# One expert's weights ahead: reordering the expert stage of a two-layer diffusion backbone, and reading its weights in longer runs

## The chip, the cores and the metric

The kernel runs on one core of one Trainium2 chip. The metric is the device time of one execution in microseconds (us). Three timed runs of the kernel before gave 2632.49, 2635.15 and 2641.01 us, a median of 2635.15 us.

## The reference, cut to what matters

Two layers work on 256 latent and 256 context tokens of width 1024. Each layer is a token mixer (differential attention, a long convolution, windowed attention, merged by gates) followed by a mixture of 16 experts. In the second layer only the 256 latent tokens go through the expert part. Each expert picks its 32 highest-scoring tokens per stream, and the expert part is:

```
def ec_moe(h, p):
    B, N, D = h.shape
    cap = CAPACITY_FACTOR * N // N_EXPERTS          # 32
    aff = softmax(h @ router_w)                     # N x 16
    g, idx = lax.top_k(swapaxes(aff, 1, 2), cap)    # per expert
    xg = take_along_axis(h, idx)                    # 16 x 32 x 1024
    a = einsum('becd,edf->becf', xg, moe_w1)
    b = einsum('becd,edf->becf', xg, moe_w3)
    y = einsum('becf,efd->becd', silu(a) * b, moe_w2) * g
    return zeros_like(h).at[flat].add(y)
```

All weights are float32. One expert has three matrices of 1024 x 1024, 12.6 MB, so a layer reads 201 MB of expert weights and the program 403 MB of its 590 MB.

## The kernel before, in words

A Python planner writes every engine's instructions in a fixed order. Foreground work (the mixer's 116 weight blocks, then the experts) is written in program order; background tasks (attention heads, convolutions, the filter of the long convolution, the modulation vectors) are generators whose steps are put between foreground matmuls when a cost model says that their inputs are ready. A `yield wait(...)` ends a step and names what the next one needs; its `gate` keeps a task back until a condition holds, for instance until a pool of tiles has a free buffer (`room`).

**Mixers.** For each block of 128 output columns TensorE does 24 matmuls of 128x512 (float32r, high and low halves). Modulation vectors 3 and 4 (shift and scale ahead of the experts) come out of background tasks, laid out as `mod[p, v, k, s]` with model row k*128+p on partition p. `router_prep` then multiplies the router weights by them.

**Ahead of the experts.** `post` transposes each of the 8 column blocks of the new hidden state to token rows (`p`), and ScalarE, VectorE and GpSimd split it into three bfloat16 parts `xr`. `gather` selects an expert group's tokens with one-hot matmuls from `xr` and gives `xg[g]`, whose partition is the position inside a block of 128 model rows.

**Experts.** In layer 0 there are two token streams, M = 64 rows per expert, NC = 2 column halves of N = 512 that share the systolic array; in layer 1 M = 32, NC = 4, N = 256. `prod` runs one product: for each of 8 blocks k of 128 model rows, NC matmuls into one PSUM tile. `expert(e)` is a chain: product with w1, silu on ScalarE into `s1`; product with w3, multiply on VectorE into `s1`; transposes of `s1` on TensorE; a copy to `aT` on VectorE; product with w2; copies of the result to `yS`. Between the matmuls of `prod` side work is written: `gather` of the next group of four experts and `scatter` of the last group, and in layer 0 from expert 5 on the filter of layer 1's long convolution.

**Weights.** `moe` cuts each matrix into two chunks of 2 MB, in the order w1, w3, w2 of each expert. A chunk holds four blocks k, and partition p of block k holds weight row k*128+p: one 4 KB row at a time, four rows 512 KB apart. `fill` issues chunks on the SP queue as long as fewer than `room` of them are held (6 at first in layer 0, 4 while the filter runs, 7 in layer 1), and is called again when `prod` has used up a chunk. A few chunks are put together from smaller buffers (`extra`, and every seventh in layer 1), with a DMA for each row block or pair. The last expert's w2 is cut by columns instead, so that its result ends in pieces.

Of the kernel before, what the change touches and what calls it, by code (L numbers as in the profile page):

```python
# [408 lines left out]
class Kernel:  # L409
# [344 lines left out]
    def mod_post(self, l, v):  # L754
        yield wait(self.modc[l][:, v])
        if v in (1, 4):
            self.mod_G(l, v)
        if v == 4:
            yield wait(self.modc[l][:, 4])
            self.router_prep(l)  # L760
            yield wait()
# [38 lines left out]
    def router_prep(self, l):  # L800
# [12 lines left out]
        self.gw[l], self.cr[l] = gw, cr  # L813

# [33 lines left out]
    def filter(self, task, l):  # L848
# [37 lines left out]
        for c0 in range(0, D, W):  # L886
# [11 lines left out]
            yield wait(ab[0])  # L898
# [8 lines left out]
            for j, op in enumerate((OP.add, OP.subtract)):  # L907
# [14 lines left out]
                yield wait(w3, dec) if j else wait()  # L922
# [123 lines left out]
    def turn(self, w, task):  # L1046
# [9 lines left out]
        return o  # L1056

# [195 lines left out]
    def hyena_gen(self, task, l, cs, u3):  # L1253
# [5 lines left out]
        yield wait(uv, gate=lambda: l in self.K and len(self.dft or ()) == 2 and self.room(a2=2)())  # L1259
        p = self.bank([128, 2, ns, 128])  # L1260
# [4 lines left out]
        uh = self.sb("a2", [128, 2, ns * 128], F32R, name="uh")  # L1265
        ul = self.sb("a2", [128, 2, ns * 128], F32R, name="ul")
# [54 lines left out]
        for j, (sa, a) in enumerate(ys):  # L1321
            yield wait(a, bank=0, gate=None if j else self.room(a2=5))
            if j == 0:
                Yf = [[self.sb("a2", [128, 2, ns * 128], F32R, name="yf") for _ in range(2)] for _ in range(2)]
            yh, yl = Yf[j]
            c = self.sb("a2", [128, 2, ns * 128], name="yc")
# [45 lines left out]
    def mixer(self, l):  # L1372
# [102 lines left out]
        def swa_in():  # L1475
            for j in range(2):
                def ev_sv(p, j=j):
                    if j == 0:
                        self.svready = set()
                        self.svt = [self.sb("a2", [128, 4, 128], name="svt") for _ in range(2)]  # L1480
# [4 lines left out]
            for g in range(2):  # L1485
                def ev_sk(p, g=g):
                    r = self.sb("a2", [128, 512], name="sk")
# [84 lines left out]
    def post(self, l, k, nq):  # L1572
# [8 lines left out]
        xr = [x[:, :, z] for x in self.xr]  # L1581
        d = self.sb("a2", [128, nq, 128], name="xd")
# [10 lines left out]
        self.acopy(xr[0], p)  # L1593
        self.tt(d, p, xr[0], OP.subtract)
# [4 lines left out]
    def moe(self, l):  # L1599
# [8 lines left out]
        chunks = []  # L1608
        for e in range(NE):
            for n in ("moe_w1", "moe_w3", "moe_w2"):  # L1610
                v = A[n][l, e].rearrange("(k p) n -> p k n", p=128)
                for hf in range(2):
                    if e == NE - 1 and n == "moe_w2":
                        chunks.append(v[:, :, hf * 512:hf * 512 + 512])
                    else:
                        chunks.append(v[:, hf * 4:hf * 4 + 4, :])
# [3 lines left out]
        extra = {4: (4, 0, 1), 7: (3, 2, 2)} if l < L - 1 else {5: (4, 0, 1), 7: (3, 2, 2)}  # L1620

        def fill(room, more=0):
            while len(self.mw) < len(chunks):
                i = len(self.mw)
                c = chunks[i]
                if i in extra:
# [4 lines left out]
                    for k in range(len(t)):  # L1631
                        nc.sync.dma_start(t[k], c[:, k])
                    if extra[i][1]:
                        t.append([self.sb("a2", [128, 512], name="mw") for _ in range(2)])
                        base += t[-1]
                        for h in range(2):
                            nc.sync.dma_start(t[-1][h], c[:, 3, h * 512:h * 512 + 512])
                elif self.held >= room:
                    return
                elif l == L - 1 and (i == 6 or i > 7 and i % 7 == 0):  # L1640
                    x = [self.sb("a8", [128, 2, D], name="mw")] + [self.sb("a4", [128, D], name="mw") for _ in range(2)]
                    nc.sync.dma_start(x[0], c[:, 0:2])
                    for k in range(2):
                        nc.sync.dma_start(x[1 + k], c[:, 2 + k])
# [6 lines left out]
                else:  # L1651
                    x = self.sb("a16", list(c.shape), name="mw")
                    nc.sync.dma_start(x, c)
# [7 lines left out]
        def body():  # L1661
# [124 lines left out]
            def prod(out, st, ws, free=True):  # L1786
                n = out.shape[1]
                m = len(ws[0])
                for k in range(KT):
# [7 lines left out]
                    if k % SIDE or not aside():  # L1797
                        self.bg.pump(0.25)

            def expert(e):  # L1800
                g, j = divmod(e, 4)
                st = lambda k: xg[g][k // 4][:, k % 4, j, :]
                w = self.mw[6 * e:6 * e + 6]
                a = self.bank([128, N])
                prod(a, st, w[0:2])
                s1 = self.sb("a2", [128, N], name="s1")
                nc.scalar.activation(s1, a, AF.Silu)
                b = self.bank([128, N])
                w = self.mw[6 * e:6 * e + 6]
                prod(b, st, w[2:4])  # L1810
                self.tt(s1, s1, b, OP.mult)
                aside()
# [181 lines left out]
```

## Time and profile before

| what | value |
|---|---|
| median of three timed runs | 2635.15 us |
| the profiled execution, and its span | 2637.57 us, 2635.8 us |
| TensorE busy | 2232.3 us, 85% of the span |
| VectorE, ScalarE, GpSimd busy | 1334.5, 883.4, 790.4 us |
| HBM read | 584.66 MB, 223 GB/s over the span |
| mean granted TensorE clock | 0.947 |

The profile page is one execution. Its span is the time from the first to the last instruction. The page cuts the span into 40 slices of 66 us; in each it gives the busy tenths of every engine, the granted TensorE clock, the busy share of the 16 DMA engines and what they moved. The same can be asked for any stretch of time; the sections below call this the table by stretches. The program has four stages: mixer 0 until about 1000 us, experts of layer 0 until 1515 us, mixer 1 until 2147 us, experts of layer 1 until the end.

### The profile page before, as it was taken

The page shows a single profiled execution, that of the slowest core. Times are in us where ns is not written, and L with a number is a line of the kernel's source. Part 1 is how long each engine was busy: PE and PEld are TensorE (multiplying, and loading weights), DVE is VectorE, ACT ScalarE, POOL GpSimd, SP SyncE. Part 2 cuts the span into 40 slices and gives each one's busy share as a digit, 9 for nine tenths or more (in the row PEclk, how much of TensorE's full clock was granted, in tenths as well). Part 3 has the DMA queues.
Part 4 walks back from the last instruction along what each step waited for, and adds up shares of the span by engine and source line. Part 5 has one row for each costly group of instructions (what it writes and reads, how often), then busy time and mean ns, then how long its engine had stood idle before and what let it go on. Part 6 is the DMA issues. An engine that isn't in the chain of part 4 may idle for free.

```text
span 2635.8 us, 38658 instructions
## 1 busy us (share of the span) xinstructions
PE 2232.3 (85%) x14938; PEld 1528.6 (58%) x14938; DVE 1334.5 (51%) x2899; ACT 883.4 (34%) x1933; POOL 790.4 (30%) x775
## 2 busy tenths in 40 slices
PE   6999898989989998998999799889888886656565
PEld 4777666767768774333343277777777763222223
DVE  4777778787672324223442068777888541111111
ACT  4445344555452242101110055545545330000001
POOL 2643435532233530001110055564554420000000
PEclk8999999999999999999999999999999988888887
DMA  8444333121213367999999953332466789999997
GB/s 292 118 118 120 93 102 114 49 59 55 64 57 95 90 247 306 373 402 404 357 376 405 400 171 89 97 88 73 118 181 190 192 309 409 409 409 409 408 409 302
DMA packets 390239, 590.31 MB, mean 224 GB/s; under 512 B 45948, under 2 KB 278056, under 8 KB 388776
## 3 DMA queue, kind: packets, MB, share of 16 engines
q1 hardware_dynamic: 390056, 587.84, 62.8%
q8 instruction: 118, 1.93, 0.3%
q14 instruction: 65, 0.53, 0.1%
HBM read 584.66 MB, written 3.15 MB: 223 GB/s over the span
## 4 chain that ended last, share of the span: by engine, by line
PE 51%; DVE 19%; DMA 19%; issue 4%; ACT 4%; SPq 2%; POOL 1%; DVEq 0%; ACTq 0%; POOLq 0%
PE p L458 47%; DMA mw<-in_moe_w_dram 16%; DVE arena L261 6%; DVE t L261 5%; PE p L469 3%; DVE wl L261 2%; SPq L261 2%; DMA wm<-in_w_mod_dram 2%; DVE qp L261 1%; ACT arena L261 1%; ACT wh L261 1%; DVE yb L261 1%; DVE yc L261 1%; DVE ma L261 1%; POOL wl L261 1%
## 5 line engine op out<-in xcount | busy, mean ns | idle before, releaser
L458 PE MATMUL p<-mw,xg 128*32 128x256 f32 (+1 forms) x3072 | 403.3, 508 | 120.5 <-DMA mw<-in_moe_w_dram 120.0
L458 PE MATMUL p<-hhi,wl 128*128 128x512 f32 (+1 forms) x1344 | 480.6, 358 | 28.0 <-DVE wl L261 27.7
L458 PE MATMUL p<-hhi,wh 128*128 128x512 f32 (+1 forms) x1344 | 496.0, 369 | 6.4 <-ACT wh L261 3.3
L458 PE MATMUL p<-hlo,wh 128*128 128x512 f32 (+1 forms) x1344 | 476.6, 355 | 2.5 <-POOL hlo L261 1.3
L261 POOL TENSOR_TENSOR wl<-wraw,wh 128x512 fp32r<-128x512 f32 x232 | 342.4, 1476 | 417.5 <-ACT wh L261 344.8
L458 PEld LDWEIGHTS p<-mw,xg 128*32 128x32 f32 (+1 forms) x3072 | 136.3, 131 | 329.6 <-issue 205.4
L458 PEld LDWEIGHTS p<-hhi,wl 128*128 128x128 f32 x1344 | 258.4, 192 | 76.1 <-DVE wl L261 41.7
L458 PEld LDWEIGHTS p<-hhi,wh 128*128 128x128 f32 x1344 | 259.4, 193 | 43.6 <-issue 10.1
L458 PEld LDWEIGHTS p<-hlo,wh 128*128 128x128 f32 x1344 | 259.6, 193 | 29.5 <-POOL hlo L261 1.9
L261 ACT ACTIVATE wh<-wraw 128x1024 fp32r<-128x1024 f32 x232 | 242.3, 1053 | 54.0 <-DMA wraw<-in_w_in_dram 14.7
L458 PE MATMUL p<-mw,aT 128*32 128x256 f32 (+3 forms) x1760 | 199.5, 469 | 67.8 <-DMA mw<-in_moe_w_dram 51.6
L261 DVE TENSOR_TENSOR wl<-wraw,wh 128x512 fp32r<-128x512 f32 x231 | 196.2, 850 | 79.4 <-ACT wh L261 73.9
L261 ACT ACTIVATE arena<-p 128x512 f32<-128x512 f32 (+1 forms) x212 | 106.7, 506 | 383.0 <-PE p L458 304.9
L261 ACT ACTIVATE yS<-p 32x256 f32<-32x256 f32 (+2 forms) x84 | 35.2, 419 | 497.3 <-PE p L458 463.8
L458 PE MATMUL p<-yb,wh 128*128 128x512 f32 (+1 forms) x768 | 197.3, 347 | 1.4 <-ACT wh L261 1.2
L261 POOL TENSOR_TENSOR sq<-sq,sq 128x512 f32<-128x512 f32 (+1 forms) x6 | 6.3, 1058 | 575.6 <-ACT sq L261 573.3
L458 PEld LDWEIGHTS p<-mw,aT 128*32 128x32 f32 (+1 forms) x1760 | 77.1, 131 | 172.9 <-issue 92.7
L261 DVE TENSOR_TENSOR s<-s,p 128x512 f32<-128x512 f32 (+1 forms) x32 | 17.7, 554 | 287.6 <-PE p L458 287.4
L261 DVE COPY yS<-p 32x512 f32<-32x512 f32 (+1 forms) x60 | 33.3, 556 | 247.1 <-ACT yS L261 247.1
L458 PE MATMUL p<-yb,wl 128*128 128x512 f32 (+1 forms) x384 | 133.3, 347 | 22.5 <-DVE wl L261 21.6
L458 PEld LDWEIGHTS p<-yb,wh 128*128 128x128 f32 x768 | 133.3, 194 | 17.3 <-ACT wh L261 1.4
L261 ACT ACTIVATE arena<-p,t 128x512 f32<-128x512 f32 (+1 forms) x192 | 116.3, 612 | 50.9 <-DVE t L261 45.7
(235 smaller groups left out, 3489.7 us busy)
## 6 DMA issues: line engine op xcount, KB each, us to landing
mw<-in_moe_w_dram SPq DMA_DIRECT2D x173, 2048.0 KB, 19.5
wraw<-in_w_in_dram SPq DMA_DIRECT2D x152, 512.0 KB, 3.9
wm<-in_w_mod_dram SPq DMA_DIRECT2D x72, 512.0 KB, 4.7
mw<-in_moe_w_dram SPq DMA_DIRECT2D x40, 512.0 KB, 15.8
mw<-in_moe_w_dram SPq DMA_DIRECT2D x17, 1024.0 KB, 22.4
wraw<-in_w_branch_dram SPq DMA_DIRECT2D x32, 512.0 KB, 3.9
wm<-in_w_mod_dram SPq DMA_DIRECT2D x5, 2048.0 KB, 7.7
wraw<-in_w_in_dram SPq DMA_DIRECT2D x32, 256.0 KB, 3.3
```

The lines of the kernel that those rows point to most:

```text
L261: return f(*args, **kw)
L458: self.nc.tensor.matmul(out, lhsT=lhsT, rhs=rhs, start=start, stop=stop, skip_group_check=tiles > 1)
L469: self.nc.tensor.transpose(out, in_, self.ident[:n, :n])
```

## The change

1. **Layout.** Chunks of w1 and w3 now put weight row p*8+k on partition p, so the four blocks of a chunk are four neighbouring rows, 16 KB in one run, with partitions 32 KB apart. Chunks of w2 put row c*N + p*nf + j on partition p (nf = 4 in layer 0, 2 in layer 1): runs of 16 KB in layer 0 and two runs of 8 KB in layer 1. The last expert's w2 keeps its cut by columns. To match, `post` writes the columns of `xr` in the new order (runs of 16 elements), the transposes of `s1` read every nf-th column, and `router_prep` brings modulation vectors 3 and 4 to the new partitions with 8 small matmuls, copies of a selection matrix, a multiply and two reductions.
2. **Order.** w1 of expert e+1 comes ahead of w2 of expert e, both in the chunk order and in TensorE's program. The transposes of `s1` of expert e are written in the middle of that w1 product (`mid`, after block 4).
3. **Pool of 8 tiles "a2".** Several gates ask for room in it, `clear` runs background steps until it has room, and in the convolution task some tiles of it are taken earlier or once instead of twice.
4. `gather` and `back` of the next group are queued at the second expert of a group, not the third, and side work is brought to its end ahead of the first product of a new group.

The diff, cut to its core:

```
+        m = self.modc[l][:, 3:5]                       # router_prep
+        p = self.bank([128, KT, 2 * KT * 2])
+        for hf in range(2):
+            sw = self.sb("a2", [128, 4, KT, 16], name="sw")
+            self.vcopy(sw, self.ident.rearrange(...)[...].to_broadcast([128, 4, KT, 16]))
+            for c in range(4):
+                self.mm(p[:, hf * 4 + c], sw[:, c].rearrange("p k q -> p (k q)"), m.rearrange("p v k s -> p (v k s)"), True, True)
+        nc.vector.reduce_sum(own, ..., axis=AX.X)
+        self.tt(t, ..., own..., OP.mult)
+        nc.vector.reduce_sum(m..., t..., axis=AX.X)
...
-        xr = [x[:, :, z] for x in self.xr]             # post
+        xr = [x.rearrange("p i (c q) -> p i c q", c=KT)[:, :, :, k * 16:(k + 1) * 16] for x in self.xr]
...
+        order = [(0, 0), (0, 1)]                       # moe
         for e in range(NE):
+            order += [(e + 1, 0), (e, 2), (e + 1, 1)] if e < NE - 1 else [(e, 2)]
+        at = {o: 2 * i for i, o in enumerate(order)}
...
+                        v = A[n][l, e].rearrange("(c p j) n -> p c j n", p=128, j=nf)
+                        chunks.append(v[:, hf * NC // 2:(hf + 1) * NC // 2])
+                else:
+                    chunks.append(A[n][l, e].rearrange("(p k) n -> p k n", p=128)[:, hf * 4:hf * 4 + 4, :])
...
-                    if k % SIDE or not aside():        # prod
+                    if mid and k == 4:
+                        mid()
+                    elif k % SIDE or not aside():
                         self.bg.pump(0.25)
...
+            def into(e, n, mid=None):
+                g, j = divmod(e, 4)
                 a = self.bank([128, N])
+                prod(a, lambda k: xg[g][k // 4][:, k % 4, j, :], weights(e, n), mid=mid)
+                if n == 0:
+                    s1s[e] = self.sb("a2", [128, N], name="s1")
+                    nc.scalar.activation(s1s[e], a, AF.Silu)
+                else:
+                    self.tt(s1s[e], s1s[e], a, OP.mult)
...
+            def turned(e):
+                    self.tr(p[:, f], s1[:, f::nf] if e < NE - 1 else s1[:, f * 128:(f + 1) * 128])
+                aTs[e] = self.sb("a2", [128, nf, 128], name="aT")
+                self.vcopy(aTs[e], p)
...
+            into(0, 0)
             for e in range(NE):
...
-                expert(e)
+                into(e, 1)
+                if e < NE - 1:
+                    if j == 3:
+                        while aside():
+                            pass
+                    into(e + 1, 0, lambda: turned(e))
+                else:
+                    turned(e)
+                outof(e)
```

TensorE in layer 0 before, an expert without side work: two chunks of w1 and two of w3 (`mw` against `xg`), the four transposes of `s1`, two chunks of w2 (`mw` against `aT`). Each row is 8 matmuls into PSUM tile `p`; the first number of a name is its buffer.

```order
L458 MATMUL p_1553_9492<-mw_1534_9343,xg_1487_8935 64x512 x8
L458 MATMUL p_1553_9492<-mw_1537_9419,xg_1488_8936 64x512 x8
L458 MATMUL p_1557_9515<-mw_1546_9447,xg_1487_8935 64x512 x8
L458 MATMUL p_1557_9515<-mw_1547_9457,xg_1488_8936 64x512 x8
L469 MATMUL p_1560_9537<-cst_1_68,s1_1556_9513 128x128 x4
L458 MATMUL p_1562_9544<-mw_1551_9476,aT_1561_9542 64x512 x8
L458 MATMUL p_1562_9544<-mw_1552_9486,aT_1561_9542 64x512 x8
```

The same place after: two chunks of w3 of expert 2, w1 of expert 3 with the transposes of expert 2 in it, w2 of expert 2, w3 of expert 3.

```order
L458 MATMUL p_1542_9448<-mw_1522_9266,xg_1484_8945 64x512 x8
L458 MATMUL p_1542_9448<-mw_1525_9342,xg_1485_8946 64x512 x8
L458 MATMUL p_1545_9470<-mw_1534_9402,xg_1484_8945 64x512 x8
L458 MATMUL p_1545_9470<-mw_1537_9419,xg_1485_8946 64x512 x2
L469 MATMUL p_1547_9483<-cst_1_68,s1_1538_9421 128x128 x4
L458 MATMUL p_1545_9470<-mw_1537_9419,xg_1485_8946 64x512 x6
L458 MATMUL p_1551_9500<-mw_1540_9432,aT_1548_9488 64x512 x8
L458 MATMUL p_1551_9500<-mw_1541_9442,aT_1548_9488 64x512 x8
```

Before, the transposes stand right behind the last w3 matmul that their operand comes from, and the first w2 matmul right behind the transposes. After, ten matmuls of another product stand between the w3 product and the transposes, and six between the transposes and w2.

The SP queue in layer 0 before, one expert's chunks (the last part is the shape as the DMA carries it, partitions first):

```order
L261 DMA mw_1534_9343<-in_moe_w1_dram 128x4x1024
L261 DMA mw_1537_9419<-in_moe_w1_dram 128x4x1024
L261 DMA mw_1546_9447<-in_moe_w3_dram 128x4x1024
L261 DMA mw_1547_9457<-in_moe_w3_dram 128x4x1024
L261 DMA mw_1551_9476<-in_moe_w2_dram 128x4x1024
L261 DMA mw_1552_9486<-in_moe_w2_dram 128x4x1024
```

After, at the same place in the queue:

```order
L261 DMA mw_1534_9402<-in_moe_w1_dram 128x4096
L261 DMA mw_1537_9419<-in_moe_w1_dram 128x4096
L261 DMA mw_1540_9432<-in_moe_w2_dram 128x4096
L261 DMA mw_1541_9442<-in_moe_w2_dram 128x4096
L261 DMA mw_1543_9457<-in_moe_w3_dram 128x4096
L261 DMA mw_1544_9467<-in_moe_w3_dram 128x4096
```

The four rows of a partition are now one run of 4096 elements, and w2 of the expert before stands between w1 and w3.

## Rows read from the trace of the kernel before

**Rows 1.** Table by stretches, both expert stages, mixers and tail.
```profile
core 0: us, PE busy (x) PEld busy (x) DVE busy (x) ACT busy (x) POOL busy (x), PEclk, DMA share, GB/s
100.00:950.00 850.00, 794.25 (x4298) 616.75 (x4297) 564.16 (x1231) 382.24 (x842) 356.27 (x350) 0.98 0.30 88
...
1050.00:1500.00 450.00, 400.50 (x2014) 154.60 (x2012) 132.75 (x298) 56.56 (x128) 36.68 (x65) 0.99 1.00 389
...
2170.00:2605.00 435.00, 265.10 (x3107) 121.31 (x3099) 49.75 (x126) 25.38 (x70) 0.00 (x0) 0.84 1.03 409
2605.00:2636.00 31.00, 19.79 (x366) 14.23 (x358) 7.85 (x25) 11.31 (x34) 2.20 (x3) 0.78 0.54 180
```
**Rows 2.** Table by stretches, parts of layer 0's experts.
```profile
1050.00:1100.00 50.00, 44.68 (x278) 18.59 (x276) 12.93 (x34) 8.66 (x22) 0.00 (x0) 1.00 0.95 366
1100.00:1150.00 50.00, 46.71 (x210) 16.54 (x207) 9.90 (x18) 3.54 (x6) 0.00 (x0) 1.00 1.02 404
...
1250.00:1300.00 50.00, 46.96 (x200) 18.64 (x198) 20.54 (x46) 4.91 (x11) 8.11 (x15) 0.95 0.92 344
...
1450.00:1500.00 50.00, 37.54 (x168) 12.06 (x170) 4.67 (x7) 3.54 (x6) 0.00 (x0) 1.00 1.02 409
```
**Rows 3.** Waits, layer 1, 2170 to 2605 us: waiter, releaser, us, times, longest.
```profile
PE p L458 <- DMA mw<-in_moe_w_dram: 154.4, 72, 4.6
...
PE p L469 <- DVE s L261: 9.5, 15, 1.0
```
**Rows 4.** TensorE's waits in layer 0, 1050 to 1500 us.
```profile
PE p L469 <- DVE s L261: 16.9, 14, 2.7
...
PE p L458 <- DMA mw<-in_moe_w_dram: 11.9, 9, 1.7
PE p L458 <- DVE aT L261: 11.0, 14, 0.8
...
PE p L458 <- POOL hx L261: 3.9, 4, 1.4
...
PE p L458 <- DVE sr L261: 2.5, 2, 1.2
```
**Rows 5.** TensorE's timeline, one expert: start, us, instruction, count, idle before.
```profile
1110.57 13.90 PE L458 MATMUL p<-mw,xg 128*64 128x512 f32 x64
1125.33 0.66 PE L469 MATMUL p<-cst,s 128*128 128x128 f32 x4 [0.86 <-DVE s L261]
1126.77 3.65 PE L458 MATMUL p<-mw,aT 128*64 128x512 f32 x16 [0.78 <-DVE aT L261]
```
**Rows 6.** Table by stretches: short stretches with other run lengths.
```profile
22.00:24.50 2.50, 2.50 (x30) 0.94 (x26) 0.42 (x1) 0.00 (x1) 0.00 (x0) 0.77 1.01 423
26.00:28.00 2.00, 1.86 (x32) 0.94 (x32) 0.86 (x3) 0.42 (x1) 0.00 (x0) 1.00 1.23 343
...
46.00:48.00 2.00, 2.00 (x8) 1.62 (x7) 2.00 (x5) 2.00 (x6) 1.10 (x2) 0.74 1.01 434
943.00:946.00 3.00, 3.00 (x15) 2.49 (x14) 0.00 (x0) 0.00 (x0) 1.26 (x2) 1.00 1.03 428
```
**Rows 7.** DMA issues: count, KB each, median us to landing; above them the packets' sizes.
```profile
DMA packets 390239, 590.31 MB, mean 224 GB/s; under 512 B 45948, under 2 KB 278056, under 8 KB 388776
...
mw<-in_moe_w_dram SPq DMA_DIRECT2D x173, 2048.0 KB, 19.5
...
xT<-spill SPq DMA_DIRECT2D x1, 2048.0 KB, 11.3
```
**Rows 8.** Groups of instructions near the added ones: busy us, mean ns.
```profile
L458 PE MATMUL p<-wr,mod 128*128 128x16 f32 x48 | 5.8, 267 | 0.0
...
L261 DVE TENSOR_TENSOR dg<-cst,t 128x512 f32<-128x512 f32 x2 | 1.4, 693 | 0.1
```
**Rows 9.** Tile xr: ns shortest, median, longest.
```profile
L261 ACT ACTIVATE xr<-p x16: 375/482/589, 960.2 to 2147.4; 128x512 bf16<-128x512 f32 x8, 128x256 bf16<-128x256 f32 x8
```
**Rows 10.** TensorE's largest wait for another engine in mixer 0, 100 to 950 us.
```profile
PE p L458 <- DVE wl L261: 26.7, 24, 4.2
```

More of the change, by code (lines that the diff above doesn't have):

```diff
@@ L758, in mod_post @@
         if v == 4:
-            yield wait(self.modc[l][:, 4])
+            yield wait(self.modc[l][:, 4], gate=self.room(a2=2))
             self.router_prep(l)
@@ L897, in filter @@
             self.tt(ab[0][:, 0], ab[0][:, 0], ab[0][:, 1], OP.add, nc.gpsimd)
-            yield wait(ab[0])
+            yield wait(ab[0], gate=self.room(a2=1))
             pn = self.bank([128, W])
@@ L921, in filter @@
                 self.tt(K[:, j, 1, c0:c0 + W], hs[:, j], hs[:, 1 - j], OP.subtract, nc.gpsimd)
-                yield wait(w3, dec) if j else wait()
+                yield wait(w3, dec) if j else wait(gate=self.room(a2=1))
         self.K[l] = K
@@ L1056, in turn, with clear @@
         return o
+    def clear(self, n):
+        while self.model.dead("a2", BUFS["a2"]) < n:
+            self.bg.force()
     def room(self, **need):
@@ L1486, in ev_sk @@
                 def ev_sk(p, g=g):
+                    self.clear(1)
                     r = self.sb("a2", [128, 512], name="sk")
@@ L1608, in moe @@
         chunks = []
+        order = [(0, 0), (0, 1)]
         for e in range(NE):
[L1610 to L1614, printed above, removed]
-                    else:
-                        chunks.append(v[:, hf * 4:hf * 4 + 4, :])
+            order += [(e + 1, 0), (e, 2), (e + 1, 1)] if e < NE - 1 else [(e, 2)]
+        at = {o: 2 * i for i, o in enumerate(order)}
+        for e, n in order:
+            n = ("moe_w1", "moe_w3", "moe_w2")[n]
+            for hf in range(2):
+                if n == "moe_w2":
+                    if e == NE - 1:
+                        chunks.append(A[n][l, e].rearrange("(k p) n -> p k n", p=128)[:, :, hf * 512:hf * 512 + 512])
+                    else:
+                        v = A[n][l, e].rearrange("(c p j) n -> p c j n", p=128, j=nf)
+                        chunks.append(v[:, hf * NC // 2:(hf + 1) * NC // 2])
+                else:
+                    chunks.append(A[n][l, e].rearrange("(p k) n -> p k n", p=128)[:, hf * 4:hf * 4 + 4, :])
         self.mw = []
```

65 lines of the change are left out of this document (36 added, 29 removed).

## The prediction

> **What bounds the kernel now.** I read the page's slices first for the four stages, then the table by stretches for each of them. In layer 1's experts the DMA engines are full from end to end: 409 GB/s at a DMA share of 1.03 over 435 us, while TensorE is busy 265 us [rows 1]. TensorE waits there for weights, 154.4 us in 72 waits, and hardly for VectorE, 9.5 us [rows 3]. The stage's length is its bytes over 409 GB/s: 435 x 0.409 = 177.9 MB. In layer 0's experts neither is full: 389 GB/s and TensorE busy 400.5 of 450 us [rows 1]. At the end of that stage the weights come at 409 GB/s; at 1250 to 1300 us, with the filter and a scatter between the products, they fall to 344 GB/s while TensorE is busy 46.96 of 50 us [rows 2]. A chunk is fetched only when TensorE has used one up, so a late TensorE becomes a missing transfer. Of what makes it late, two waits belong to the chain inside an expert: for the multiplied `s` 16.9 us and for `aT` 11.0 us, 27.9 us in 14 experts [rows 4]. In the timeline of one expert they are the 0.86 us idle ahead of the transposes and the 0.78 us ahead of the w2 product [rows 5]. The mixers are TensorE's: busy 794 of 850 us with DMA at 88 GB/s [rows 1], so nothing done to the weights shortens them.
>
> **Longer runs, layer 1.** The chunks' rate is what this stage is made of. Rates of other run lengths stand in short stretches: modulation weights with 8 KB rows came at 423 GB/s over 2.5 us, the reload of the hidden state in 16 KB runs at 428 GB/s over 3 us, its spill at 434 GB/s [rows 6]. The 1463 packets of 8 KB and more in the page's count (390239 less 388776) say that a long run does travel as one long packet [rows 7], and the order shows the rows of a partition as one run of 4096 elements: that the change fails to do what it says is unlikely. By the code, 85 chunks (177.9 MB over 2.1 MB) will be 49 in 16 KB runs, 24 of w2 in 8 KB runs, and 12, every seventh, half in 8 KB and half in 4 KB runs. That is 102.8 MB at 428, 62.9 MB at 423 and 12.6 MB at 409 GB/s: 240.1 + 148.7 + 30.8 = 419.6 us for 178.3 MB, 418.7 us for 177.9 MB. The stage loses 16 us. Bounds: 435 us if the rate stays (0), 410 us at 434 GB/s throughout (25 less). The 31 us after it [rows 1] are pieces of the last w2, which keeps its cut: unchanged.
>
> The Trainium skill, "DMA: Bandwidth & Descriptors", section "Why small descriptors are slow", gives each packet a fixed cost of about 3 cycles beside one beat per 32 bytes. By that 4 KB is 128 + 3 and 16 KB is 512 + 3, and the rate would rise by 1.7% alone, to an estimated 416 GB/s; the rows' 428 over 409 is 4.6%. The sum by the rule would be 2615 us.
>
> **Layer 0.** Bytes: 450 x 0.389 = 175.05 MB, nearly all in 16 KB runs after, so 175.05 / 0.428 = 409 us is the floor set by transfers; at 409 GB/s it is 428 us. TensorE's floor is its 400.5 us of work and the waits that the new order does not touch, 3.9 us for the filter's `hx` and 2.5 us for `sr` [rows 4]: 407 us. The 27.9 us of waits for `s` and `aT` go: 64 instructions of `mw` against `xg`, two to a matmul, took 13.90 us, 0.43 us a matmul [rows 5]; the transposes now stand ten matmuls, 4.3 us, behind the w3 product, whose multiplied result was 0.86 us late, and w2 stands six, 2.6 us, behind the transposes, where `aT` was 0.78 us late. What is late next is the weights. If VectorE is held up by filter work, the transposes wait in the middle of w1, and the rest of w1 and w2 queue behind them; the longest such wait was 2.7 us [rows 4], still under the 4 us. The two floors are nearly equal, so neither hides the other wholly. Before, the stage took 22 us more than its higher floor (428); with a good half of TensorE's idle time gone I take 13. 409 + 13 = 422 us, 28 less. Bounds: 409 (41 less), and 440 (10 less) if most of the waits come back in another place. The SP queue has as many issues as before, one queue, and the chunks are used in the order in which they are fetched, so no issue is moved past one that TensorE needs earlier.
>
> **What is added.** `router_prep` gets 8 matmuls in each layer, float32, two instructions each: 32 at 5.8/48 = 0.12 us, by the nearest group [rows 8], is 4 us, in mixers where TensorE is the path. Its four copies and two multiplies on VectorE at 0.69 us [rows 8] lie beside matmuls, VectorE being busy 564 of 850 us [rows 1]; uncovered they would cost another 4 us. The writes of `xr` in runs of 16 elements: 0.59 us each before [rows 9]; if they took twice that, only those of the last column block of each layer stand on the path, two or three of 0.6 us. I take 1 us (0 to 3). The gates and `clear` write background steps in another order through both mixers. TensorE's work there is the same but for the 16 matmuls; what can change is what it waits for. Its largest wait for another engine in mixer 0, for `wl`, is 26.7 us [rows 10]: bounds of 27 us either way, of which I take 0, as there is no reason for either sign. Together 5 us more.
>
> **Sum.** The profiled execution took 2637.57 us, 1.8 us around its span, 2.4 us above the median of the timed runs and inside their spread. 2637.6 - 28 - 16 + 5 = 2598.6 us; less 2.4 us, 2596 us.
>
> **Rivals.**
> *The rate of a long stream stays at 409 GB/s*, the rates of rows 6 being bursts of 2 MB. For it: no row shows more than 5 us above 409 GB/s. Against: 8 KB and 16 KB bursts agree among themselves, and the 4 KB stream shows no sign of tiring over 435 us. Layer 1 then gains nothing; layer 0 has 428 us of transfers and a TensorE floor 21 us below, which halves the 13: 434 us, 16 less. 2637.6 - 16 + 5 - 2.4 = 2624 us. Chance 15%.
>
> *Layer 0 is kept by TensorE.* Two experts' `s1` and `aT` now live in the pool of 8 tiles "a2" together with the gather's, the filter's and the scatter's tiles, and the filter asks for room there: a wait for a buffer takes the place of the wait for `s`. For it: the rate of 344 GB/s where all of these meet [rows 2]. Against: the order holds no forced block of filter steps. Stage at 440 us: 2637.6 - 10 - 16 + 5 - 2.4 = 2614 us. Chance 20%.
>
> *Rows 32 KB apart are slow to read.* Partitions of w1 and w3 now begin 32 KB apart, all of them at one power of two. The reload of rows 6 had its partitions 16 KB apart, as w2 of layer 0 will; no row shows 32 KB. Two thirds of 352.95 MB are at stake. With 5 us of work added and 5 us of collision, the kernel breaks even where transfers take 875 us, a mean of 403 GB/s; with w2 at 425 that is 393 GB/s for w1 and w3. Below that it is slower: at 343 GB/s, the rate of a mixed stretch with the engines full [rows 6], 235.3/0.343 + 117.65/0.425 + 10 = 973 us against 885, 88 more: 2723 us. Chance 8%.
> The Trainium skill, "DMA: Bandwidth & Descriptors", section "Latency and other measured facts", lists slow copies at row pitches of large powers of two, from 207 of 214 GB/s at 512 KiB down to 103 at 4 MiB. This pitch lies below its list, and no row here bears on it; hence a small chance.
>
> *The background steps of the mixers fall badly*, the largest wait there more than doubled: 40 us more than the sum, 2636 us. Chance 5%.
>
> **How the numbers follow.** The forecast has 52%, with a range of its own from 2580 to 2612 us (its bounds in layer 0, a few us of layer 1 and of the mixers). To hold 8 in 10 the range takes in both milder rivals and a mixer that gains or loses half of its bound: 2566 to 2626 us. A change under 0.3%, 8 us, can't be told from none. Faster: 51 of the forecast, 12 of the first rival, 18 of the second, 3 of the others: 84%. Same: 8%. Slower: 8%, nearly all of it the pitch.
>
> **What would show it.** Layer 1's stage at 422 to 430 GB/s instead of 409 and TensorE's waits there still for `mw`; a rate of 409 to 416 means the first rival, below 400 the third. In layer 0 no waits for `s` and `aT`, and a rate above 410 GB/s also with the filter; waits of VectorE, or of TensorE for `hx` and `s`, at below 400 GB/s mean the second. Page sizes: most bytes in packets of 8 KB and more. Mixers within 10 us of 850 and their total. I am wrong if the stages keep their length though the rate in full stretches has risen, or if the mixers move by more than the experts.

## The result, and the profile after

The changed kernel took 2604.8 us (median of four runs, 2602.67 to 2612.82) beside 2637.41 us for the kernel before in the same comparison: a ratio of 0.9883, 95% interval 0.9856 to 0.9911. It is faster by 1.2%, and the interval leaves out a ratio of 1. The forecast was 2596 us with a range of 2566 to 2626.

The profiled execution took 2604.43 us, its span 2602.7 us. The stages are cut here at the first matmul of w1 and the last of w2 of each layer, by their starts in TensorE's timeline:

| stage | before, us | after, us | difference | forecast |
|---|---|---|---|---|
| mixer 0 | 1027.8 | 1019.9 | -7.9 | +5 with mixer 1 |
| experts, layer 0 | 493.7 | 477.7 | -16.0 | -28 |
| mixer 1 | 643.1 | 648.7 | +5.6 | (in the +5) |
| experts, layer 1 | 458.2 | 443.2 | -15.0 | -16 |
| tail | 13.0 | 13.1 | +0.1 | 0 |
| span | 2635.8 | 2602.7 | -33.1 | -39 |

The table by stretches of the changed kernel (columns as in rows 1): mixer 0, layer 0's experts, layer 1's experts.

```profile
100.00:950.00 850.00, 802.18 (x4365) 627.73 (x4363) 573.21 (x1246) 384.70 (x845) 363.76 (x355) 0.99 0.31 91
1050.00:1500.00 450.00, 413.81 (x2093) 164.18 (x2093) 137.75 (x308) 61.81 (x139) 41.90 (x69) 0.99 0.98 399
2160.00:2565.00 405.00, 256.75 (x2940) 114.44 (x2929) 47.77 (x122) 24.20 (x66) 0.00 (x0) 0.82 1.01 423
```

Against [rows 1], layer 1's rate rose from 409 to 423 GB/s with the DMA engines still full (share 1.01) and TensorE still well below the length of the stretch. Layer 0's rose by less, from 389 to 399, and TensorE is now busy 414 of 450 us there instead of 400.5.

TensorE's waits after, layer 1 (2160 to 2565 us) and then layer 0 (1030 to 1480 us): waiter, releaser, us, times, longest.

```profile
PE p L458 <- DMA mw<-in_moe_w_dram: 144.2, 76, 4.4
PE p L469 <- DVE sg L261: 1.7, 1, 1.7
```
```profile
PE p L458 <- DMA mw<-in_moe_w_dram: 20.8, 21, 2.0
PE p L458 <- POOL hx L261: 6.4, 4, 3.5
PE p L469 <- DVE sg L261: 2.9, 4, 2.2
PE p L458 <- DVE sr L261: 2.2, 2, 1.1
```

In layer 1 the weights are what ends nearly all of TensorE's waits, as before [rows 3]; the 9.5 us for `s` are gone. In layer 0 the waits for `s` and `aT`, 27.9 us in [rows 4], are gone from the list. Those for weights rose from 11.9 to 20.8 us: a third of what the chain gave back is now spent waiting for transfers.

Layer 0's experts cut in four, first of before, then of the changed kernel (same columns; before's first part starts at 1028 us, where its stage starts).

```profile
1028.00:1108.00 80.00, 71.32 (x402) 27.46 (x402) 19.16 (x54) 12.24 (x30) 0.00 (x0) 1.00 0.91 351
1108.00:1250.00 142.00, 129.05 (x656) 49.05 (x654) 41.25 (x92) 18.21 (x41) 7.55 (x12) 0.99 1.03 404
1250.00:1450.00 200.00, 182.87 (x888) 72.81 (x884) 72.53 (x164) 26.15 (x59) 29.13 (x53) 0.98 0.98 380
1450.00:1512.00 62.00, 46.47 (x214) 15.51 (x216) 6.05 (x9) 3.54 (x6) 0.00 (x0) 1.00 1.03 405
```
```profile
1020.00:1100.00 80.00, 77.58 (x424) 29.83 (x426) 19.05 (x54) 12.94 (x32) 0.00 (x0) 0.98 0.85 349
1100.00:1250.00 150.00, 137.25 (x688) 51.69 (x686) 39.26 (x88) 17.91 (x40) 6.83 (x11) 1.00 1.01 423
1250.00:1450.00 200.00, 186.26 (x906) 73.96 (x904) 75.83 (x169) 27.29 (x62) 29.93 (x54) 0.99 0.99 397
1450.00:1490.00 40.00, 33.52 (x162) 12.38 (x158) 4.83 (x7) 2.24 (x4) 0.00 (x0) 0.96 1.02 411
```

This is the table to read the result from. Where the DMA engines are full (1100 to 1250) the rate is 423 GB/s, as in layer 1. In the first 80 us and from 1250 to 1450 us it is far below, and TensorE is busy 97% and 93% of the time: there TensorE uses up chunks more slowly than they could come. In the first 80 us the rate did not rise at all (351, 349).

From 1250 to 1450 us the DMA share of 0.99 is a mean that hides where the loss sits. Two stretches in it, of the changed kernel:

```profile
1280.00:1320.00 40.00, 38.58 (x250) 17.56 (x246) 15.77 (x42) 9.07 (x24) 4.45 (x8) 1.00 0.94 362
1420.00:1440.00 20.00, 18.18 (x80) 7.30 (x82) 6.95 (x16) 1.67 (x4) 4.75 (x9) 0.91 0.90 340
```

Against 428 GB/s they fall short by 40 x (428 - 362)/428 = 6.2 us and 20 x (428 - 340)/428 = 4.1 us. In the first, TensorE is busy nearly throughout at a granted clock of 1.00 (2.4 GHz). In the second the clock fell: from 1414 to 1420 us TensorE was busy 2.81 of 6 us, and from 1422 to 1424 us the granted clock was 0.50 (1.2 GHz). So a part of the loss is the clock's and not the amount of work; the runs don't separate the two there.

The place behind 1250 us in TensorE's timeline, the changed kernel: start, us, instruction, count, idle before.

```profile
1253.01 1.08 PE L458 MATMUL p<-mw,xg 128*64 128x512 f32 x4 [1.32 <-DMA mw<-in_moe_w_dram]
1254.02 1.13 PE L458 MATMUL p<-sgt,yS 128*128 128x256 f32 x4
1255.08 1.94 PE L458 MATMUL p<-mw,xg 128*64 128x512 f32 x8
1256.95 1.13 PE L458 MATMUL p<-sgt,yS 128*128 128x256 f32 x4
1258.01 1.08 PE L458 MATMUL p<-mw,xg 128*64 128x512 f32 x4
1259.02 0.49 PE L458 MATMUL p<-arena,ones 128*128 128x128 f32 x2
1259.44 1.08 PE L458 MATMUL p<-mw,xg 128*64 128x512 f32 x4
1260.45 1.13 PE L458 MATMUL p<-sgt,yS 128*128 128x256 f32 x4
...
1287.87 1.03 PE L458 MATMUL p<-mw,xg 128*64 128x512 f32 x4
1288.83 1.51 PE L458 MATMUL p<-S,xr 128*128 128x128 bf16 x24
```

`sgt,yS` is the scatter, `arena,ones` the filter, `S,xr` the gather. From this first w3 matmul to that of the next expert (1287.87) pass 34.86 us, with hardly any idle time; an expert's 12.58 MB at 428 GB/s are 29.4 us. The gather follows at once, and the next expert is as slow (its successor's w3 begins at 1322.79).

DMA on the page of the changed kernel: packets by size, and the first row of the issues.

```profile
DMA packets 325983, 590.31 MB, mean 227 GB/s; under 512 B 45948, under 2 KB 278056, under 8 KB 297896
...
mw<-in_moe_w_dram SPq DMA_DIRECT2D x173, 2048.0 KB, 20.7
```

28087 packets (325983 less 297896) are now of 8 KB and more, where [rows 7] had 1463; the count of issues is the same.

### The profile page after: what moved, and what is told of

Read it like the earlier page. It is cut to its first block, busy times and chain, and to the rows that moved or that the text cites. A ratio compares the mean times of both kernels' runs of the same rounds, so it can differ in the third digit from the quotient of the medians.

```text
span 2602.7 us, 38721 instructions
## 1 busy us (share of the span) xinstructions
PE 2240.1 (86%) x14970; PEld 1538.0 (59%) x14970; DVE 1339.4 (51%) x2909; ACT 884.2 (34%) x1933; POOL 793.1 (30%) x775
## 2 busy tenths in 40 slices
DMA packets 325983, 590.31 MB, mean 227 GB/s; under 512 B 45948, under 2 KB 278056, under 8 KB 297896
## 4 chain that ended last, share of the span: by engine, by line
PE 49%; DMA 23%; DVE 19%; ACT 3%; issue 3%; POOL 2%; SPq 1%; DVEq 0%; ACTq 0%; POOLq 0%
PE p L458 46%; DMA mw<-in_moe_w_dram 20%; DVE arena L261 6%; DVE t L261 5%; PE p L469 3%; DVE wl L261 2%; DVE qp L261 2%; DMA wm<-in_w_mod_dram 1%; DMA wraw<-in_w_in_dram 1%; ACT wh L261 1%; DVE yb L261 1%; ACT arena L261 1%; SPq L261 1%; POOL wl L261 1%; DVE yc L261 1%
## 5 line engine op out<-in xcount | busy, mean ns | idle before, releaser
L458 PE MATMUL p<-mw,xg 128*32 128x256 f32 (+1 forms) x3072 | 411.6, 508 | 120.0 <-DMA mw<-in_moe_w_dram 118.4
L458 PEld LDWEIGHTS p<-hlo,wh 128*128 128x128 f32 x1344 | 261.0, 194 | 29.4 <-POOL hlo L261 1.6
L261 ACT ACTIVATE s<-p 128x512 f32<-128x512 f32 (+1 forms) x32 | 15.7, 491 | 346.2 <-PE p L458 346.1
```

Of the source, the lines that this page charges most:

```text
L261: return f(*args, **kw)
L458: self.nc.tensor.matmul(out, lhsT=lhsT, rhs=rhs, start=start, stop=stop, skip_group_check=tiles > 1)
```

## The experiments

### The two parts apart

*Layout alone*: the old order of products and chunks, the old queueing of `gather`, all the rest of the change.

```
-        order = [(0, 0), (0, 1)]
-        for e in range(NE):
-            order += [(e + 1, 0), (e, 2), (e + 1, 1)] if e < NE - 1 else [(e, 2)]
+        order = [(e, n) for e in range(NE) for n in (0, 1, 2)]
```

> The changed kernel with the layout in long runs and the edits of the tile pool, but the experts in the old order (w1, w3, transposes, w2 of one expert, chunks in that order, gather queued at the third expert). Stages are measured from the first w1 matmul to the last w2 matmul: layer 0 493.7 us before and 477.7 us after, layer 1 458.2 and 443.2 us. My theory (layer 1 is all transfer rate; layer 0 is kept by TensorE's heavy stretches, which its lookahead of four chunks does not cover): layer 1 443 us as after, with 423 GB/s; layer 0 about 488 us, since the waits for s and aT (28 us) are back; in all about 2617 us. If the order made layer 1's gain, layer 1 stays at 458 us. If the rate alone made layer 0's gain, layer 0 is 478 us.

*Order alone*: the old chunks, `xr`, transposes and `router_prep`, all the rest of the change, the earlier queueing of `gather` included.

```
-                    chunks.append(A[n][l, e].rearrange("(p k) n -> p k n", p=128)[:, hf * 4:hf * 4 + 4, :])
+                    chunks.append(A[n][l, e].rearrange("(k p) n -> p k n", p=128)[:, hf * 4:hf * 4 + 4, :])
```

> The changed kernel with the experts in the new order and the edits of the tile pool, but the weights, xr, the transposes of s1 and router_prep in the old layout (4 KB rows). My theory: layer 1 458 us at 409 GB/s; layer 0 about 483 us, with its waits for s and aT gone and transfers at 409 GB/s as the next bound; mixers about 5 us shorter than after, since router_prep has no permutation; in all about 2620 us. If layer 0's gain comes from the rate, layer 0 stays near 494 us. If long runs slow something else down, this kernel is as fast as the changed one.

*The pool edits alone*: both reverted, part 3 of the change kept.

> The kernel before with part 3 of the change alone: the gates on the pool of 8 tiles and the moved tiles in the convolution, with the old order, the old layout and no added work in router_prep. My theory: part 3 writes the background steps of mixer 0 in a poorer order (the kernel with part 2 and 3 had mixer 0 at 1040.6 us, 12.8 above before, with no other difference there), and the new work in router_prep happens to push them back. Then mixer 0 is 1040 us, layer 0's experts 494, mixer 1 643, layer 1's experts 458: 2650 us, a ratio of 1.005. Rival: the 12.8 us came with the new order of chunks, whose first transfers start in mixer 0. Then mixer 0 is 1028 us and the total 2638 us, a ratio of 1.000.

| kernel | median, us (range) | ratio, interval | mixer 0 | layer 0 | mixer 1 | layer 1 |
|---|---|---|---|---|---|---|
| layout alone | 2621.1 (2616.06 to 2623.16) | 0.9924, 0.9906 to 0.9941 | 1018.4 | 492.5 | 651.0 | 443.8 |
| order alone | 2647.12 (2643.74 to 2652.46) | 1.0029, 1.0018 to 1.004 | 1040.6 | 490.0 | 643.3 | 458.3 |
| pool edits alone | 2647.12 (2643.74 to 2648.58) | 1.003, 1.0018 to 1.0042 | 1040.4 | 487.2 | 645.1 | 458.1 |
| all (the change) | 2604.8 (2602.67 to 2612.82) | 0.9883, 0.9856 to 0.9911 | 1019.9 | 477.7 | 648.7 | 443.2 |

Layer 1's two stretches, of layout alone and then of order alone (columns of rows 1):

```profile
2175.00:2585.00 410.00, 257.35 (x2984) 118.67 (x2984) 48.76 (x124) 24.91 (x68) 0.00 (x0) 0.83 1.01 423
```
```profile
2185.00:2605.00 420.00, 263.49 (x2953) 117.22 (x2949) 47.74 (x122) 24.54 (x67) 0.00 (x0) 0.81 1.03 409
```

Layer 1 follows the layout alone: 423 GB/s with it in the old order, 409 in the new order without it. Three expectations were missed: layer 0 took 492.5 us with layout alone (488 expected), 490.0 with order alone (483) and 487.2 with the pool edits alone (494), and order alone was 27 us slower in all than expected (2620), most of it in mixer 0.

In layer 0 neither part does much by itself: against the 493.7 us before, all three kernels are within 7 us, and the whole change takes 16 off. The kernel with the pool edits alone is the nearest to compare with, as all of them have these edits. From its 487.2 us, order adds 2.8, layout adds 5.3, and both together take 9.5 off; the other 6.5 of the 16 us came with the pool edits. The single numbers of 3 to 6 us are not to be relied on, since TensorE's clock differs between the profiles. The stage of the pool edits alone and of layout alone, the same work (columns of rows 1):

```profile
1040.40:1527.60 487.20, 435.14 (x2220) 169.85 (x2220) 144.00 (x327) 65.27 (x146) 39.48 (x68) 1.00 1.00 389
1018.40:1510.90 492.50, 445.78 (x2219) 174.42 (x2220) 143.96 (x327) 65.16 (x146) 39.48 (x68) 0.98 0.96 384
```

For the same instructions TensorE is busy 10.6 us longer in the second, whose clock falls to its lower level six times. The 9.5 us are not of this kind: the changed kernel has TensorE busy longer (441.8 us) than the pool edits alone and is the faster one. TensorE's waits show why. With layout alone (first rows, 1050 to 1500 us) the chain's waits stand and the weights are hardly waited for; with order alone (last row) the chain's are gone and the weights take their place:

```profile
PE p L469 <- DVE s L261: 12.6, 15, 0.9
PE p L458 <- DVE aT L261: 11.8, 15, 0.8
...
PE p L458 <- DMA mw<-in_moe_w_dram: 5.6, 5, 1.3
```
```profile
PE p L458 <- DMA mw<-in_moe_w_dram: 29.7, 24, 1.9
```

A floor is here the shortest time that a resource by itself allows the stage. Layout alone lowers the transfers' floor, while TensorE's, with its waits, stays where it was; order alone lowers TensorE's, while the transfers' stays.

In mixer 0 the pool edits cost 12.6 us, with nothing else changed (1040.4 against 1027.8), and the kernels that also have the new `router_prep` stand at 1017 to 1022 us in the profiles of all eleven. More than half of the 20.5 us between the pool edits alone and the changed kernel lies in one stretch, first with the pool edits alone, then the changed kernel at its like place:

```profile
507.00:584.00 77.00, 59.50 (x308) 46.77 (x307) 55.00 (x140) 38.72 (x102) 23.87 (x25) 0.87 0.14 35
```
```profile
490.00:567.00 77.00, 71.03 (x353) 58.17 (x353) 58.64 (x116) 44.60 (x102) 38.80 (x37) 0.98 0.24 62
```

TensorE is idle 17.5 of 77 us there without the new `router_prep`, 6 with it. The 16 matmul records and a few VectorE steps that it adds stand long before, at 325 us; what they change, by the way the planner works, is which background steps it finds ready later; no run has `router_prep` alone. In mixer 1 the same addition shows as a price: 647 to 655 us in all with it, 643 to 645 without.

### The pitch of the rows

The forecast's third rival was that partitions 32 KB apart are slow to read. Here each chunk of w1 and w3 is 2 MB in one piece, partitions 16 KB apart.

```
-    rearrange("(p k) n -> p k n", p=128)[:, hf * 4:hf * 4 + 4, :]
+    rearrange("(c p k) n -> p c k n", c=2, k=4)[:, hf]
```

> The changed kernel, but a chunk of w1 and w3 is read as one contiguous piece of 2 MB: runs of 16 KB at a pitch of 16 KB from partition to partition instead of 32 KB. The weight rows then meet the wrong rows of x, so the products are not the reference's; the amount of work is the same. If the pitch of 32 KB costs nothing: the same time within 0.3%, 423 GB/s in layer 1. If the pitch costs something (the rival of slow reading): layer 1's rate rises to 428 or more and its 443 us fall by 4 us or more; layer 0 likewise if its 399 GB/s come from the pitch.

2607.56 us (2603.19 to 2608.37), ratio 0.9872 (0.9856 to 0.9888). The table by stretches, layer 0 and layer 1:

```profile
1050.00:1490.00 440.00, 405.64 (x2043) 159.07 (x2044) 133.03 (x300) 56.38 (x129) 36.68 (x65) 0.99 0.98 401
2160.00:2565.00 405.00, 256.19 (x2924) 116.71 (x2920) 47.74 (x122) 23.97 (x66) 0.00 (x0) 0.83 1.01 423
```

The same 423 GB/s, the same stage (443.0 us): between 16 and 32 KB the pitch makes no difference here. The Trainium skill, "DMA: Bandwidth & Descriptors", section "Latency and other measured facts", lists slow pitches from 512 KiB up, for copies between HBM tensors; this trace neither contradicts nor extends that, since nothing was slow at 16 and 32 KB.

### Transposes in the middle of the next product, or at once

```
-                    into(e + 1, 0, lambda: turned(e))
+                    turned(e)
+                    into(e + 1, 0)
```

> The changed kernel with the transposes of s1 right behind the w3 product, ahead of the next w1 product and not in the middle of it; the order of the products and of the chunks stays. It brings back the wait for s (0.86 us before each transposes' group and up to 2.7 us where the filter holds VectorE; 16.9 us in 14 experts of layer 0 in the trace of before), but not the wait for aT. If layer 0 is bound by TensorE's lateness as I hold: 477.7 us becomes some 488 us. If its transfers are the bound by themselves: 478 us still. Layer 1, which waits for weights: 443 us either way. In all 2604 to 2616 us.

2610.43 us (2608.25 to 2614.43), ratio 0.989 (0.987 to 0.9911). Its waits in layer 0, 1050 to 1500 us:

```profile
PE p L469 <- DVE s L261: 14.1, 15, 2.7
PE p L458 <- DMA mw<-in_moe_w_dram: 10.1, 10, 1.7
```

The wait for `s` is back with 14.1 us, but the stage is only 3 us longer (480.7), and the wait for weights is some 12 us shorter than the changed kernel's in the same stretch (22.0). My theory had 488 and the rival 478: neither. By this run a microsecond of waiting removed from TensorE is worth about a fifth of one; the shorter wait for weights says that most of the rest was spent while a chunk was on its way. Two things blur the fifth: 3 us are within what the clock moves between profiles, and block 4 of the w1 product goes back to side work here. Layer 1 took 445.1 us, 2 more than expected.

### What holds the rate down in layer 0

*Side work at every fourth block of a product, not every second*; the second kernel does it in layer 0 alone.

```
-SIDE = 2
+SIDE = 4
```

> The changed kernel with SIDE = 4 instead of 2: one step of side work (gather, scatter) in every fourth block of a product instead of every second, so that the scatter and the gather of a group are spread over some three experts, not one and a half. My theory for layer 0's shortfall (heavy stretches of TensorE longer than the lookahead, so that transfers run dry, and light ones in which TensorE waits for weights): layer 0 falls from 478 to about 465 us, rate in 1250 to 1350 us above 410 GB/s; layer 1 unchanged at 443; in all about 2592 us. Rival (the transfers of layer 0 are slow in themselves, or TensorE's total work is the bound): layer 0 unchanged within 3 us.

> The version with side work in every fourth block, but in layer 0 alone; layer 1 keeps every second. Layer 0 465.7 us as in that version, layer 1 443 us (there 445.4). If mixer 1's length (652.5 us there, 648.7 us after) hangs on how layer 0 ends, it stays as there. In all about 2592 us; 2594 if layer 1's 2 us were scatter.

*At every third block* (SIDE = 3).

> The changed kernel with a piece of side work at every third block of a product (SIDE 3), where the changed kernel has every second (477.7 us in layer 0's experts) and a kernel run earlier every fourth (465.7 us). My theory, that the spacing of side work decides between the two floors: 468 to 474 us in layer 0, total 2593 to 2600 us. Rival: SIDE 4 was better because the transposes already stand at block 4 and take the place of one side piece there, so that only a multiple of 4 thins the pieces out within that product; then SIDE 3 stays at 476 to 479 us.

*The gather queued at the third expert of a group, as before.*

```
-                if j == 1 and g < 3:
+                if j == 2 and g < 3:
```

> The changed kernel with the gather of the next group queued at the third expert of a group, as before, and not at the second. My theory is that layer 0 loses transfers where scatter, gather and filter steps stand back to back in one expert, since TensorE then takes longer for a chunk than its transfer lasts. Queued later, the gather has two experts less of room but stands clear of the scatter, which is queued at the first: I expect 1250 to 1450 us to rise from 397 towards 410 GB/s and layer 0's experts to take 470 to 475 us in place of 477.7. Rival: the amount of side work is what counts, not its spacing; then the gather, pressed into one expert and what is forced out at the end of the group, costs the same, and the stage stays at 477 to 480 us, or gets longer through the forced part. Layer 1: 443 us by both.

*Without the filter's work*, with room for 4 chunks and then for 6.

```
-                    self.bg.add("filter", lambda task: self.filter(task, l + 1), 4)
```

> The changed kernel without the filter of layer 1's convolution in the expert stage of layer 0: the filter's work is left out (its table is set to zero, so layer 1's convolution is wrong), while the number of chunks held stays at 4 from expert 5 on, as with the filter. Some 25 us of TensorE work are gone from layer 0. Theory (heavy stretches of TensorE longer than the lookahead): layer 0 falls from 477.7 to about 465 us, with dips left where scatter and gather stand. If transfers bound it by themselves: 478 us.

> As the last one (the filter's work left out, layer 1's convolution wrong), but with 6 chunks held instead of 4 until expert 13. Theory: the longer lookahead covers the heavy stretches of scatter and gather, so that transfers run full at 415 to 425 GB/s from 1100 us on and layer 0 falls by some 5 to 10 us more, to about 457 us. If lookahead doesn't matter: as the kernel without the filter and 4 chunks, within 2 us.

*SIDE = 4 and the later gather together.*

> Two edits at once on the changed kernel: side work at every fourth block (SIDE 4) and the gather of the next group queued at the third expert of a group. Alone, SIDE 4 gave 465.7 us in layer 0's experts, and moved 420 GB/s instead of 397 from 1250 to 1450 us; the late gather gave 472.5 us, with 388 GB/s instead of 349 from 1020 to 1100 us and no gain from 1250 to 1450. My theory: the two work in different places and add up in part, 460 to 464 us for the stage, some 2589 us in total, because the late gather stays clear of the first 80 us. Rival: with five side pieces an expert, the gather queued at the third expert doesn't get done in the ten places left, and what is forced out in one piece ahead of the next group takes back what the start gains; then 465 to 472 us and a total at or above the 2594 us of SIDE 4 alone.

| kernel | median, us (range) | ratio, interval | layer 0, us | layer 1, us |
|---|---|---|---|---|
| SIDE 4 | 2593.74 (2587.93 to 2601.35) | 0.9821, 0.9792 to 0.985 | 465.7 | 445.4 |
| SIDE 4, layer 0 alone | 2594.9 (2590.31 to 2602.29) | 0.9837, 0.9812 to 0.9862 | 465.7 | 445.3 |
| SIDE 3 | 2604.6 (2602.95 to 2607.77) | 0.9874, 0.9849 to 0.9899 | 478.3 | 443.1 |
| later gather | 2598.68 (2594.58 to 2602.77) | 0.9854, 0.9822 to 0.9887 | 472.5 | 443.1 |
| no filter, room 4 | 2581.03 (one run) | | 456.6 | 442.5 |
| no filter, room 6 | 2586.01 (one run) | | 456.6 | 442.9 |
| SIDE 4 and later gather | 2587.56 (2585.57 to 2592.09) | 0.9808, 0.978 to 0.9835 | 462.4 | 445.4 |

The two slow parts of the stage in four kernels, by stretches: SIDE 4; the later gather; both; no filter with room 4 (its first row starts at 1100 us).

```profile
1250.00:1450.00 200.00, 191.66 (x934) 75.59 (x932) 72.43 (x159) 25.71 (x58) 25.50 (x46) 0.99 1.01 420
1020.00:1100.00 80.00, 75.41 (x406) 29.22 (x404) 17.64 (x48) 10.73 (x25) 0.00 (x0) 0.96 0.90 365
```
```profile
1250.00:1450.00 200.00, 185.28 (x909) 74.01 (x910) 73.48 (x164) 26.56 (x60) 29.79 (x54) 0.99 0.98 398
1020.00:1100.00 80.00, 76.22 (x416) 29.52 (x414) 16.69 (x44) 11.13 (x25) 0.00 (x0) 0.98 0.94 388
```
```profile
1250.00:1450.00 200.00, 190.05 (x940) 75.66 (x938) 74.28 (x164) 26.67 (x60) 29.15 (x53) 1.00 1.01 415
1020.00:1100.00 80.00, 76.50 (x419) 29.50 (x415) 15.47 (x41) 11.13 (x25) 0.00 (x0) 0.98 0.94 396
```
```profile
1100.00:1250.00 150.00, 135.96 (x668) 50.22 (x664) 28.51 (x60) 15.14 (x33) 0.00 (x0) 0.99 1.01 428
1250.00:1450.00 200.00, 178.26 (x855) 65.72 (x856) 39.66 (x82) 16.36 (x36) 2.31 (x1) 1.00 1.01 427
```

How many chunks are under way shows the same. The issues of 2 MB chunks from 1250 to 1450 us, with the median time from issue to landing in us: the changed kernel, then no filter with room 4.

```profile
mw<-in_moe_w_dram SPq DMA_DIRECT2D x38, 2048.0 KB, 10.5
mw<-in_moe_w_dram SPq DMA_DIRECT2D x40, 2048.0 KB, 20.6
```

One chunk at 428 GB/s takes 4.9 us, so by this estimate about two are under way in the changed kernel and four, the whole room, without the filter. If the transfers were slow in themselves, the landing would take longer in the slower kernel, not shorter.

Five things follow. SIDE 4 lifts 1250 to 1450 us from 397 to 420 GB/s with the same work (2220 TensorE instructions in the stage in both): an expert with scatter and filter then takes 30.98 us (1249.64 to 1280.62) instead of 34.86, since by the code 5 places for side work stand in it instead of 11 (blocks 0 and 4 of three products, less the one that the transposes take, against blocks 0, 2, 4 and 6, less one); in the timeline above the scatter fills 8 of the 11. SIDE 3 missed: I had 468 to 474 us and it took 478.3, as its rival said (476 to 479). Counted by the code it leaves 9 places of 11, and in the product with the transposes 3 of 3, where SIDE 4 leaves 1; I hadn't counted. The later gather gave the stage that I expected but not where: 1250 to 1450 stayed at 398, and the first 80 us went from 349 to 388 GB/s, 3.1 MB or 7 us earlier. The earlier queueing in the change's part 4 thus cost about 5 us. With the filter gone the rate is 427 to 428 from 1100 to 1450 us, with no dips left, and the stage takes 456.6 us where I expected 465. Two more chunks of room then change nothing (456.6 both; 5 to 10 us expected, a miss). As the transfers were full already with room 4, that run can't say whether more room would help beside the filter; this rival is untested. Why it is 420 with SIDE 4 and not 427, with the engines full in both (share 1.01), is open; SIDE 4 also carries the filter's own ten reads of 64 and 128 KB there, which the other kernel leaves out. The two good edits add up in part: 462.4 us against 465.7 with SIDE 4 alone, in a profile with a slightly higher clock (1.00 against 0.99 over the stage), and 2587.56 us in all, with overlapping ranges. It is the lowest median among the kernels that compute the reference's result. Layer 1 takes 2 us more with SIDE 4 even where only layer 0 has it (443 was expected); why is open.

## Why the prediction was right, and where it was not

**Layer 1: right in mechanism and size.** 16 us less forecast, 15 measured, 423 GB/s in the stretch; with the weights still the bound, and the same gain from the layout alone. The forecast mixture of 428, 423 and 409 gave 425. The Trainium skill, "DMA: Bandwidth & Descriptors", section "Why small descriptors are slow", gave an estimated 416 GB/s; the trace has 423, more than its fixed cost per packet accounts for. With the length of the runs one more thing changed: the four rows of a partition were 512 KB apart and are now neighbours. No run separates the two. The rival of a rate that stays at 409 is out: the rates of the short stretches [rows 6] hold for 400 us.

**Layer 0: right in mechanism, mis-sized.** The step that failed is "with a good half of TensorE's idle time gone I take 13": the collision above the 409 us floor. The stage lost 16 us instead of 28, so the term was 25, not 13. The cause is how it was formed: I set two floors for the whole stage, 409 us of transfers and 407 of TensorE, and took half of the old collision. By the four parts of the stage, the time in which bytes were missing against 428 GB/s is 80 x (428 - 349)/428 = 14.8 us at the start, 14.5 from 1250 to 1450, and 3.3 in the two others, 33 in all. Before, against its own 409, the same sum is 11.3, 14.2 and 2.3, 28 us. It did not fall; it grew, as in the two crowded parts TensorE's pace sets the rate and faster transfers help next to nothing: order alone, with its 4 KB runs, reaches nearly the same rate at the like place (its stage begins 20 us later) as the changed kernel's 397.

```profile
1270.00:1470.00 200.00, 181.50 (x886) 71.50 (x885) 75.52 (x170) 27.40 (x62) 31.04 (x56) 0.99 1.02 392
```

The waits of the chain went as forecast, but where the transposes stand at once 14.1 us of them cost only 3. That the crowding sets the rate from 1250 to 1450 us is shown: thin out the side work and the rate there is 420, take the filter away and it is 427. At the start of the stage only the gather's part is shown (349 to 388 GB/s). What the falls of the clock add is seen but not separated. Two smaller flaws of the term: the floor of 407 us leaves out the 2.7 us of waits for `sg`, which stayed (2.9 after), and 1050 to 1500 us leaves out the first 22 us of the stage, among its slowest (307 GB/s from 1027.8 to 1050 us in the trace of before).

**The rival "layer 0 is kept by TensorE"** had the right engine and rate (below 400 GB/s with the filter) and the wrong reason: among TensorE's waits none for a buffer of the pool took the place of that for `s`; what releases TensorE in layer 0, weights aside, adds up to 11.5 us (`hx` of the filter, `sg` and `sr` of the steps around the gather). It is TensorE's own work, standing too close together.

**Mixers: price right, total not.** The 8 added matmuls, 16 records, take 1.94 us in the timeline of layer 1, so 3.9 us in both layers where 4 was forecast; `sw` is copied in 0.61 us; and the `xr` writes in runs of 16 elements take a median of 483 ns where [rows 9] had 482: the 1 us taken for them was nothing. The tile `sw` and its matmuls in the changed kernel, and `xr` (ns shortest, median, longest):

```profile
L458 PE MATMUL p<-mod,sw x32: 267/320/402, 325.5 to 2003.7; 128*128 128x32 f32 x32
L261 DVE COPY sw<-cst x4: 610/614/617, 324.7 to 2001.8; 128x512 f32<-128x512 f32 x4
```
```profile
L261 ACT ACTIVATE xr<-p x16: 376/483/590, 952.5 to 2129.2; 128x512 bf16<-128x512 f32 x8, 128x256 bf16<-128x256 f32 x8
```

But the reordered background, taken at 0 with 27 us either way, was not 0: it is +12.6 us for the pool edits and -20.5 us when the rest of the change, `router_prep` in it, comes on top (1040.4 to 1019.9; order alone stays at 1040.6), which nets to -7.9 in mixer 0. The bound of 27 held. Why this order of steps is the better one is not shown by any run; it is the planner's luck, and that luck hid 7 us of the miss in layer 0: -33.1 us measured against -39 is 12 short in layer 0, 7 better in the mixers, 1 short in layer 1.

**The pitch** of 32 KB, given 8%, is out by the 423 GB/s of the changed kernel itself and by the experiment with 16 KB.

## What to carry to other kernels

Where two floors are nearly equal, price a change part by part of the stage: faster transfers count only in the parts in which they bind, and here lowering either floor alone left the stage at 490 to 492.5 us while lowering both brought it to 477.7. Look then at how the remaining work is spread, since one number (side work at every fourth block) gave 12 us more. And when a static planner writes the background, an edit to its gates can move other stages, here by 12.6 us up and 20.5 us down: keep that in the range, and separate it by a run with those edits alone. Before a stage of one profile is compared with that of another, compare the granted clock and the busy time of the same instructions.

## What the runs showed of the hardware that was not expected

A stream of 2 MB reads was the faster the longer its runs, and held its rate: 409 GB/s in 4 KB runs over 420 us, 423 with 16 and 8 KB mixed over 405 us, 427 to 428 nearly all in 16 KB over 350 us. (The 4 KB runs of a partition also lay 512 KB apart; no run tells which of the two counts.) Half the pitch between partitions made no difference to it. A write in runs of 16 bfloat16 elements on ScalarE cost what a straight one did, 483 against 482 ns.

TensorE's clock fell in the middle of a busy stage. In layer 0's experts with layout alone it went from 1.00 to 0.50 (2.4 to 1.2 GHz) six times, for 3 to 4 us each, every time right behind a stretch in which TensorE had been idle for a part; the same work took 445.8 us of busy time there and 435.1 us in the profile in which the clock stayed at 1.00.
